# Layer 0's MLP output on the seven-product scheme, its sums added up by transfers, modulation loads moved

## The chip, the cores and the metric

The kernel runs on one core of a Trainium2 chip. The metric is the device time of one execution in microseconds (us). Three runs of the kernel before took 2149.72, 2150.34 and 2150.58 us, median 2150.34. A difference is called measurable here where it is over 0.2% of that, 4.3 us.

A core has engines that work side by side, each through its own instruction queue in order: TensorE (PE, matrix products into the banks of PSUM), VectorE (DVE, element-wise work), ScalarE (ACT, element-wise functions), GpSimd (POOL) and SyncE (SP). The last two do little here but start transfers (DMAs).

## The reference

A two-layer encoder trunk on one sequence of 256 tokens with 2048 features, all in float32. Only its shape matters:

```python
for l in range(2):
    mod = silu(c) @ w_ada[l] + b_ada[l]                 # 2048 x 12288
    sh_a, sc_a, g_a, sh_m, sc_m, g_m = split(mod, 6)
    h = rmsnorm(x) * (1 + sc_a) + sh_a
    x = x + g_a * (attention(h) @ w_o[l])               # two groups of heads
    h = rmsnorm(x) * (1 + sc_m) + sh_m
    y = square(relu(h @ w_mlp_in[l])) @ w_mlp_out[l]    # 2048 -> 8192 -> 2048
    x = x + g_m * y
return rmsnorm(x, final_norm_g)
```

## The kernel before

**Products in parts.** A float32 matrix is split into `hi` (rounded to float32r by ACT) and `lo` (the rest, subtracted by DVE), and a product is three: hi by hi, hi by lo, lo by hi. So each weight tile of 128 by 2048 numbers (1 MB) that SP loads into a `raw` buffer costs ACT two roundings and DVE two subtractions of 128 by 1024 (`weights`, `part`, L151 and L154) before PE can use it. There are five `raw` buffers and four each of `hi` and `lo`, so loads and splits run ahead of PE by about two tiles of weights.

**The MLP.** The 8192 hidden features are worked off in four blocks (`fb` 0 to 3) of 2048. A block first makes its hidden features 128 at a time (`wides`, PE tile `ps`, L217 and L220; then `relu2` or `relu` and `split`), then multiplies them with 2048 rows of the second matrix. That second product gives 2048 output columns, in four column groups `c` of 512, for two halves `t` of the tokens. `rows` and `rows_by_k` (PE tile `pr`, L311 to L314) make one column group from four weight tiles, with 96 products of 128 by 512.

Layer 0 does so for all four column groups (`mlp`). Block 0 keeps its results in `y`, block 1 adds them (`added`), and `updates` multiplies each result with the gate row (`row`, tile `bias`) into `yg` and adds it to `x` on DVE.

Layer 1 (`block_by_seven`) makes the left half (column groups 0 and 1) differently: two by two blocks (token halves by feature halves by column groups) are multiplied with seven block products in place of eight, by sums and differences of blocks. `seven` makes the combinations for each pair of feature tiles: of the hidden features (`comb`, `sh`, `sl`) and of the weights (`comb`, 128 by 2048, L1179 to L1181). It adds its products into seven PSUM banks `pp`, p1 to p7, in two steps, `five` and `two`, that are placed between the `wides` of later tiles. At the end of a block `four` combines p1 to p7 into the four results on DVE. The right half stays with `rows_by_k`. So a block of layer 1 has two stages: one that mixes `ps` and `pp`, and one of `pr` alone (8 weight tiles, 192 products).

**Modulation.** `mod` is computed on DVE: 192 tiles of `w_ada` of 1 MB each, each multiplied and summed by one instruction (`ada_sums`, L380). The loads go through the same queue (SP) and the same five `raw` buffers as the weights. How many are started is set by `rate`: each call of `weights` adds `rate` to a credit and starts that many loads; the sums stand on DVE behind the next weight tile's splits. `ada_need` makes sure that a group is there when it is used.

**The order.** Instructions of each engine stand in program order but for what a scheduler in the recording layer exchanges, so places are shown below as the built program has them.

Of the kernel before, what the change touches and what calls it, by code (L numbers as in the profile page):

```python
# [18 lines left out]
D = 2048  # L19
# [78 lines left out]
RATE_A0, RATE_V, RATE_A1, RATE_A2, RATE_K, RATE_K1, RATE_M = 1.1, 1.6, 0.5, 0.7, 0.6, 0.0, 0.7  # L98
# [3 lines left out]
class Trunk:  # L102
    def __init__(self, ctx, tc, io):
# [4 lines left out]
        self.up = pool("up", 40)  # L108
        self.tp = pool("tp", 6)
# [190 lines left out]
    def rows_by_k(self, pss, w, xs, kq, ts=(0, 1)):  # L300
# [3 lines left out]
        for h in range(2):  # L304
            for i in range(4):
                for t in ts:
                    ps = pss[t].rearrange("p a b -> p (a b)")
                    c = slice(t * P, (t + 1) * P)
                    xh, xl, _ = xs[4 * kq + i]
# [572 lines left out]
    def layer(self, l, acc=None):  # L882
# [164 lines left out]
        self.rate = RATE_M  # L1047
        if l:
            for fb in range(NFB):
                self.block_by_seven(fb, h, banks)  # L1050
                banks = []
        else:
            self.mlp(h, banks)
        self.quiet = False

    def mlp(self, h, banks):

        io = self.io
        late = []
        for fb in range(NFB):  # L1060
            hid = []
            done = 0 if fb else 12
            for m in range(done, NK, 2):
                ps = self.wides([io["w_m10"][NK * fb + m + j - 12] for j in range(2)], h)
                for b in banks:
                    hid += self.relu2(b)
                banks = []
                hid += self.relu2(self.joined(ps, self.t("sum")))
            if fb == 1:
                self.gate(0, 5)  # L1070
            for c in range(4):
                pss = self.rows(io["w_m2"][0, fb], hid, c, fb == NFB - 1 and c == 3)
                if fb == 0:
                    late += [self.copy(ps, "y") for ps in pss]
                else:
                    if late:
                        pss = [self.added(late.pop(0), ps) for ps in pss]
                    self.updates(pss, c, fb == NFB - 1)

    def block_by_seven(self, fb, h, banks):  # L1080
# [3 lines left out]
        plain = len(banks)  # L1084
        for m in range(0, plain, 2):
            hid += self.relu2(self.joined(banks[m : m + 2], self.t("sum")))
        for m in range(plain, NK, 2):
            both = self.t("sum")
            for j in range(2):
                ps = self.wides([io["w_m11"][NK * fb + m + j - 6]], h)[0]  # L1090
                self.join(ps, both[:, j])
                if m > plain + 2:
                    steps.pop(0)()
            r = self.relu(both)
            parts = self.split(r, "hid", True)
            hid += parts
            steps += self.seven(io["w_ms"][fb, m // 2], parts, r, sums, m == plain, m == NK - 2)
        for f in steps:
            f()
        if fb == 0:  # L1100
            self.gate(1, 5)
        end = fb == NFB - 1
        done = self.final if end else self.updates
        first, adds, halves = self.four(sums)
        first()
        light = adds + [lambda c=c: done(halves[c], c) for c in range(2)]
        pss = [self.bank("pr") for _ in range(2)]
        for kq in range(4):
            self.rows_by_k(pss, self.weights(io["w_m2"][1, fb, 2, kq]), hid, kq)
            if kq < 3 or not plain:  # L1110
                light.pop(0)()
        done(pss, 2)
        if plain:
            self.both_by_k([self.weights(io["w_ms"][fb, m // 2]) for m in range(0, plain, 2)], hid, halves)
            light.pop(0)()
        if end:
            light.pop(0)()
            pss = self.rows(io["w_m2"][1, fb], hid, 3, True)
        else:
            pss = [self.bank("pr") for _ in range(2)]  # L1120
            for kq in range(4):
                self.rows_by_k(pss, self.weights(io["w_m2"][1, fb, 3, kq]), hid, kq)
                if light:
                    light.pop(0)()
        done(pss, 3)

    def both_by_k(self, ws, xs, halves):
# [15 lines left out]
        for c in range(2):  # L1143
            for t in range(2):
                y = flat(halves[c][t])
# [514 lines left out]
```

## Time and profile before

| | us |
|---|---|
| Runs (three): lowest, median, highest | 2149.72, 2150.34, 2150.58 |
| Profiled execution, first to last instruction (its span) | 2147.8 |
| Layer 0, attention and first norm (to the first `tx` of the MLP's norm) | 0 to 398 |
| Layer 0, MLP: norm and block 0; block 1; block 2; block 3 | 398 to 581; to 757; to 933; to 1109 |
| Layer 1, attention | 1109 to 1445 |
| Layer 1, MLP: norm and block 0; block 1; block 2; block 3 | 1445 to 1623; to 1795; to 1967; to 2139 |

The profile tells no time of its execution other than the span; the 2.5 us by which the median of the runs is longer lie around it. The stages are read from the timeline of PE, by the names of its output tiles. Matrix products overlap in their pipeline: a product of 128 by 512 is shown with 0.39 us, but the next starts 0.23 us later; the same holds in part for DVE and ACT.

### The profile page before, as it was taken

What the parts mean: (1) busy time and instruction counts of PE and PEld (TensorE: products, weight loads), DVE (VectorE), ACT (ScalarE), POOL (GpSimd) and SP (SyncE); (2) the same over time, 40 slices, a digit from 0 to 9 for tenths busy, and PEclk for the clock granted to TensorE, in tenths of its full rate; (3) what the DMA queues carried; (4) which work ended last, traced back from release to release, by engine and by line L of the source; (5) the groups of instructions that cost most, each with busy time, mean ns of one, the idle gap of its engine ahead of it and who ended that gap; (6) DMA issues with size and microseconds to landing.
All of it is one profiled execution on the core that took longest, in us unless ns stands there. A gap on an engine that the chain in (4) does not pass through costs nothing.

```text
span 2147.8 us, 29564 instructions
## 1 busy us (share of the span) xinstructions
PE 2122.2 (99%) x11411; PEld 1841.3 (86%) x11411; DVE 1776.3 (83%) x2444; ACT 1209.9 (56%) x1829; POOL 6.2 (0%) x18
## 2 busy tenths in 40 slices
PE   7999999999999999999999999999999999999998
PEld 6899887898888888888889998888888888888886
DVE  8889888988688888888877886778977897897897
ACT  6555663565465355345455576647645765664674
POOL 0000000000000000000000000000000000000000
PEclk9999999999999999999999999999999999999999
DMA  9989899799888888988967776776665564565553
GB/s 395 423 343 334 324 353 346 285 335 344 322 318 329 347 319 323 341 311 318 344 222 275 255 254 236 274 250 210 227 237 186 184 239 153 198 233 177 191 191 128
DMA packets 87245, 594.76 MB, mean 277 GB/s; under 512 B 9856, under 2 KB 10304, under 8 KB 20288
## 3 DMA queue, kind: packets, MB, share of 16 engines
q1 hardware_dynamic: 85536, 586.41, 73.9%
q0 software_dynamic: 848, 5.28, 0.6%
q8 instruction: 89, 1.46, 0.3%
q10 hardware_dynamic: 720, 1.19, 0.2%
q14 instruction: 52, 0.43, 0.1%
HBM read 589.66 MB, written 3.18 MB: 276 GB/s over the span
## 4 chain that ended last, share of the span: by engine, by line
PE 92%; DVE 3%; DMA 2%; ACT 2%; issue 1%; ACTq 0%; DVEq 0%
PE ps L217 19%; PE pr L311 10%; PE pr L314 10%; PE pr L312 10%; PE ps L220 10%; PE pk L260 3%; PE pk L284 2%; PE pk L194 2%; PE pk L198 2%; PE pk L197 2%; PE pp L1171 2%; PE pp L1170 2%; PE pp L1172 2%; PE pv L298 2%; PE pv L296 2%; PE pv L297 2%
## 5 line engine op out<-in xcount | busy, mean ns | idle before, releaser
L151 ACT ACTIVATE hi<-raw 128x1024 fp32r<-128x1024 f32 (+2 forms) x714 | 720.1, 1019 | 617.0 <-PE pr L312 275.6
L154 DVE TENSOR_TENSOR lo<-raw,hi 128x1024 fp32r<-128x1024 f32 (+2 forms) x714 | 821.1, 1171 | 261.8 <-issue 105.5
L380 DVE SCALAR_TENSOR_TENSOR ada<-ada,cond 128x2048 f32<-128x2048 f32 x192 | 438.2, 2284 | 13.8 <-DMA ada<-in_w_ada 13.1
L217 PE MATMUL ps<-h,hi 128*128 128x512 f32 x1856 | 436.5, 390 | 0.0
L217 PEld LDWEIGHTS ps<-h,hi 128*128 128x128 f32 x1856 | 345.2, 188 | 71.1 <-DVE sum L1367 1.3
L311 PE MATMUL pr<-hi,hid 128*128 128x512 f32 x768 | 298.9, 389 | 0.0
L312 PE MATMUL pr<-hi,hid 128*128 128x512 f32 x768 | 298.8, 389 | 0.0
L220 PEld LDWEIGHTS ps<-h,lo 128*128 128x128 f32 x1856 | 234.2, 191 | 6.8
L220 PE MATMUL ps<-h,lo 128*128 128x256 f32 x1856 | 236.2, 283 | 0.0
L314 PE MATMUL pr<-lo,hid 128*128 128x512 f32 x768 | 190.3, 389 | 0.0
L312 PEld LDWEIGHTS pr<-hi,hid 128*128 128x128 f32 x768 | 144.2, 188 | 29.9
L314 PEld LDWEIGHTS pr<-lo,hid 128*128 128x128 f32 x768 | 144.1, 188 | 29.9
L311 PEld LDWEIGHTS pr<-hi,hid 128*128 128x128 f32 x768 | 144.1, 188 | 29.8
L1366 ACT ACTIVATE sum<-ps 128x256 f32<-128x256 f32 x110 | 42.0, 382 | 87.4 <-PE ps L220 86.8
L194 PE MATMUL pk<-h,hi 128*128 128x256 f32 x320 | 90.4, 285 | 0.2 <-ACT h L715 0.2
L198 PE MATMUL pk<-h,lo 128*128 128x256 f32 x320 | 90.5, 283 | 0.0
L197 PE MATMUL pk<-h,hi 128*128 128x256 f32 x320 | 90.5, 283 | 0.0
L260 PE MATMUL pk<-hf,w 128*128 128x256 f32 x384 | 83.9, 379 | 0.0
L260 PEld LDWEIGHTS pk<-hf,w 128*128 128x128 f32 x384 | 72.8, 190 | 9.9
L154 DVE TENSOR_TENSOR lo<-comb,hi 128x1024 fp32r<-128x1024 f32 x58 | 70.4, 1218 | 6.3 <-PE ps L220 6.3
L151 ACT ACTIVATE hi<-comb 128x1024 fp32r<-128x1024 f32 x58 | 60.7, 1052 | 8.5 <-PE pp L1172 5.5
L194 PEld LDWEIGHTS pk<-h,hi 128*128 128x128 f32 x320 | 61.2, 192 | 0.6 <-ACT h L715 0.5
(288 smaller groups left out, 3129.2 us busy)
## 6 DMA issues: line engine op xcount, KB each, us to landing
raw<-in_w_m SPq DMA_DIRECT2D x206, 1024.0 KB, 5.9
ada<-in_w_ada SPq DMA_DIRECT2D x192, 1024.0 KB, 6.5
raw<-in_w_o SPq DMA_DIRECT2D x32, 1024.0 KB, 5.7
raw<-in_w_ms SPq DMA_DIRECT2D x32, 1024.0 KB, 5.0
raw<-in_w_m SPq DMA_DIRECT2D x24, 768.0 KB, 5.4
raw<-in_w_dv SPq DMA_DIRECT2D x16, 1024.0 KB, 5.8
raw<-in_w_t SPq DMA_DIRECT2D x12, 1024.0 KB, 5.0
w<-in_w_a SPq DMA_DIRECT2D x24, 384.0 KB, 13.5
```

The source lines that it names most:

```text
L151: ins = self.nc.scalar.activation(hi, v, AF.Copy)
L154: ins = self.nc.vector.tensor_tensor(lo, v, hi.bitcast(F32), ALU.subtract)
L194: ins = mm(ps, hi, x[0], start=first, stop=False, skip_group_check=shared)
L197: mm(ps, hi, x[1], start=False, stop=False, skip_group_check=shared)
L198: self.last_mac = mm(ps, lo, x[0], start=False, stop=last, skip_group_check=shared)
L217: mm(ps.rearrange("p a b -> p (a b)"), part(w, k, 0), x[2], start=k == 0, stop=False)
L220: mm(ps[:, 0], part(w, k, 1), x[0], start=False, stop=k == nk - 1)
L260: self.nc.tensor.matmul(ps, v, whole[k], start=first, stop=last, skip_group_check=True)
L311: mm(ps, xh[:, c], part(i, 0), start=kq == 0 and i == 0, stop=False)
L312: mm(ps, xl[:, c], part(i, 0), start=False, stop=False)
L314: self.last_mm = mm(ps, xh[:, c], part(i, 1), start=False, stop=kq == 3 and i == 3)
L380: ins = nc.vector.scalar_tensor_tensor(w, w, 1.0, self.cond, ALU.mult, ALU.mult, accum_out=acc[:, i : i + 1])
```

## The change

- **Layer 0, blocks 1 to 3** go through `block_by_seven`: the left half of the second product by seven block products, as in layer 1. Block 0 (`first_block`) stays with `rows`.
- **The sums p1 to p7 are kept over the blocks** of a layer in seven tiles `acc` in the memory SBUF, and combined once, at the end of block 3 (`merged`, seven additions on DVE). In the blocks between, ACT copies each bank into a tile `part`, and a transfer that POOL starts adds it to `acc` (`gather`); in block 3 DVE adds the banks (`gather` with `end`). Block 0's left half goes into `acc` as p2, p3, p4, p7 (layer 0: by copies and one subtraction; layer 1: by `both_by_k`, as before for the tiles that `wide_by_k` made).
- **Gated rows of the right half** are multiplied with the gate on DVE and added to `x` by such a transfer (`add_late`), for blocks 1 and 2 and, in the next block's first stage, for block 0. Block 3 adds on DVE (`updates`, `final`), the left half of all blocks with it.
- **Modulation loads** start at other rates: none in the `ps`/`pp` stages of layer 0, 1.25 for each weight tile in the `pr` stages, 1.0 in block 0, more in layer 1's attention (0.7 and 1.2 for 0.5 and 0.7), 0.3 in the first stage of layer 1's block 0.
- Hidden features are split in one instruction of 512 columns in place of two of 256. Pools: `u` 44 for 40 tiles, `t` 8 for 6; the memory for transfers that POOL starts shrinks to 4096 bytes of each partition.

```diff
-RATE_A0, RATE_V, RATE_A1, RATE_A2, RATE_K, RATE_K1, RATE_M = 1.1, 1.6, 0.5, 0.7, 0.6, 0.0, 0.7
+RATE_A0, RATE_V, RATE_A1, RATE_A2, RATE_K, RATE_K1, RATE_M0, RATE_R = 1.1, 1.6, 0.7, 1.2, 0.6, 0.4, 1.0, 1.25
+RATE_S = 0.0, 0.3
...
-        if l:
-            for fb in range(NFB):
-                self.block_by_seven(fb, h, banks)
-                banks = []
-        else:
-            self.mlp(h, banks)
+        acc, late = ({}, []) if l else self.first_block(h, banks)
+        for fb in range(1 - l, NFB):
+            self.block_by_seven(l, fb, h, banks if l and fb == 0 else [], acc, late)
...
     def block_by_seven(self, l, fb, h, banks, acc, late):
...
+            if fb == 1 and m == 2:
+                self.gate(l, 5)
+            while m > 4 and late:
+                self.add_late(*late.pop(0))
...
+        self.rate = RATE_R
         end = fb == NFB - 1
-        done = self.final if end else self.updates
-        first, adds, halves = self.four(sums)
-        first()
-        light = adds + [lambda c=c: done(halves[c], c) for c in range(2)]
+        light = [lambda g=g: self.gather(acc, sums, g, end) for g in ((1, 2), (3, 5), (7, 6), (4,))]
+        halves = []
+        if end:
+            done = self.final if l else lambda pss, c: self.updates(pss, c, True)
+            light += [lambda: halves.extend(self.merged(acc))]
+            light += [lambda c=c: done(halves[c], c) for c in range(2)]
+        elif fb:
+            def done(pss, c):
+                for t in range(2):
+                    self.add_late(pss[t], t, c)
...
+    def gather(self, acc, sums, group, end):
+        flat = lambda v: v.rearrange("p a b -> p (a b)")
+        for i in group:
+            ps = sums[i - 1]
+            if i not in acc:
+                acc[i] = self.copy(ps, "acc")
+            elif end:
+                self.nc.vector.tensor_tensor(acc[i], ps, acc[i], ALU.add)
+            else:
+                t = self.t("part")
+                self.nc.scalar.activation(t, ps, AF.Copy)
+                self.nc.gpsimd.dma_start(flat(acc[i]), flat(t), accum_op=ALU.add)
+
+    def add_late(self, y, t, c):
+        tmp = self.t("yg").rearrange("p a b -> p (a b)")
+        self.nc.vector.tensor_tensor(
+            tmp, y.rearrange("p a b -> p (a b)"), self.row[:, 512 * c : 512 * c + 512], ALU.mult
+        )
+        self.nc.gpsimd.dma_start(self.xs_of(t, c), tmp, accum_op=ALU.add)
+
+    def merged(self, acc):
+        op = self.nc.vector.tensor_tensor
+        a1, a2, a3, a4, a5, a6, a7 = [acc[i] for i in range(1, 8)]
+        op(a6, a1, a6, ALU.add)
+        op(a2, a1, a2, ALU.add)
+        op(a7, a6, a7, ALU.add)
+        op(a4, a7, a4, ALU.subtract)
+        op(a6, a6, a5, ALU.add)
+        op(a3, a6, a3, ALU.add)
+        op(a5, a7, a5, ALU.add)
+        return [a2, a4], [a3, a5]
...
-        return self.split(self.relu(ps), "hid", True)
+        return self.split(self.relu(ps), "hid")
...
-    nc = bacc.Bacc("TRN2", target_bir_lowering=False, num_devices=1)
+    nc = bacc.Bacc("TRN2", target_bir_lowering=False, num_devices=1, dynamic_dma_scratch_size=4096)
```

**DVE, last stage of layer 0's block 3.** These rows of the kernel before stand in the middle of the stage, between two weight tiles (`lo` are the splits of weights, `ada` the sums of the modulation, `yg` and `x` the gated update):

```order
L154 TENSOR_TENSOR lo_9358<-raw_9355,hi_9357 128x1024
L154 TENSOR_TENSOR lo_9362<-raw_9355,hi_9361 128x1024
L154 TENSOR_TENSOR lo_9406<-raw_9403,hi_9405 128x1024
L154 TENSOR_TENSOR lo_9410<-raw_9403,hi_9409 128x1024
L380 SCALAR_TENSOR_TENSOR ada_9365,macc_94<-ada_9365,cond 128x2048
L394 TENSOR_TENSOR mod_93<-macc_94,vec 128x2
L154 TENSOR_TENSOR lo_9444<-raw_9441,hi_9443 128x1024
L1288 TENSOR_TENSOR yg_9391<-pr_9243,bias 128x512
```

At the same place the changed kernel has, between the last split of one weight tile and the first of the next (`acc` are the kept sums):

```order
L155 TENSOR_TENSOR lo_9782<-raw_9775,hi_9781 128x1024
L381 SCALAR_TENSOR_TENSOR ada_9748,macc_88<-ada_9748,cond 128x2048
L1160 TENSOR_TENSOR acc_6645<-acc_6553,acc_6645 128x512
L395 TENSOR_TENSOR mod_87<-macc_88,vec 128x2
L1161 TENSOR_TENSOR acc_4852<-acc_6553,acc_4852 128x512
L1162 TENSOR_TENSOR acc_5010<-acc_6645,acc_5010 128x512
L1303 TENSOR_TENSOR yg_9820<-acc_4852,bias 128x512
L1163 TENSOR_TENSOR acc_4854<-acc_5010,acc_4854 128x512
L1164 TENSOR_TENSOR acc_6645<-acc_6645,acc_6601 128x512
L1305 TENSOR_TENSOR x<-x,yg_9820 128x512
L1165 TENSOR_TENSOR acc_5008<-acc_6645,acc_5008 128x512
L1166 TENSOR_TENSOR acc_6601<-acc_5010,acc_6601 128x512
```

Ahead of the next weight tile now stand the merge, part of the update of the left half, and a modulation sum. From the stage's last `sl` split to the split `lo_9942` in its next-to-last weight tile, DVE's queue holds 15 splits of weights of 128 by 1024, 7 modulation sums, 26 additions and multiplications of 128 by 512 (7 `gather`, 7 `merged`, 12 for `yg` and `x`) and 4 small ones; between the first uses of the same two tiles PE's queue holds 173 products of 128 by 512.

**SP, last stage of a middle block in layer 0.** Loads of the kernel before, in block 2:

```order
L170 DMA raw_6242<-in_w_m 128x2048
L364 DMA ada_6253<-in_w_ada 128x2048
L170 DMA raw_6279<-in_w_m 128x2048
L170 DMA raw_6325<-in_w_m 128x2048
L364 DMA ada_6335<-in_w_ada 128x2048
```

and of the changed kernel, at the beginning of that stage in block 2:

```order
L171 DMA raw_8109<-in_w_m 128x2048
L365 DMA ada_8119<-in_w_ada 128x2048
L365 DMA ada_8121<-in_w_ada 128x2048
L171 DMA raw_8153<-in_w_m 128x2048
L365 DMA ada_8166<-in_w_ada 128x2048
L171 DMA raw_8198<-in_w_m 128x2048
L365 DMA ada_8209<-in_w_ada 128x2048
L171 DMA raw_8238<-in_w_m 128x2048
```

Overall, the queue of SP starts 88 modulation loads in layer 0's MLP before and 56 now (28 with block 0 and the norm, 10, 10 and 8 in the `pr` stages), 28 in layer 1's attention before and 47 now (17 of them with the 16 tiles of `w_o`, before 10), and 2 in layer 1's MLP before and 15 now, in its norm and block 0; layer 0's attention keeps its 74.

**POOL, same stage.** Before, POOL's queue has only the gate rows here; now, for block 2 of layer 0:

```order
L1146 DMA acc_6553<-part_8101 128x512
L1146 DMA acc_4852<-part_8104 128x512
L1146 DMA acc_5008<-part_8147 128x512
L1146 DMA acc_6601<-part_8150 128x512
L1146 DMA acc_5010<-part_8192 128x512
L1146 DMA acc_6645<-part_8195 128x512
L1146 DMA acc_4854<-part_8235 128x512
L1154 DMA x<-yg_8276 128x512
L1154 DMA x<-yg_8279 128x512
L1154 DMA x<-yg_8437 128x512
L1154 DMA x<-yg_8440 128x512
```

Eleven transfers of 256 KB that add to what lies at their target now run beside that stage's 18 loads of 1 MB; block 1 has eight.

113 lines of the change are left out of this document (47 added, 66 removed).

## The prediction

> **What bounds the kernel now.** I read the page's busy times and its chain of waits first, then the stages by windows, then the order of work in time at the places that the change touches. The page (busy time, share of the span, instructions; then the chain's shares by engine):
>
> ```profile
> PE 2122.2 (99%) x11411; PEld 1841.3 (86%) x11411; DVE 1776.3 (83%) x2444; ACT 1209.9 (56%) x1829; POOL 6.2 (0%) x18
> ...
> PE 92%; DVE 3%; DMA 2%; ACT 2%; issue 1%; ACTq 0%; DVEq 0%
> ```
>
> PE is busy in 99% of the span and carries 92% of the chain, so time is saved only where PE gets fewer or shorter products, and lost wherever something makes PE wait. DVE with 83% is the engine with the least to spare. The windows by stage (length, busy us and instructions of PE, PEld, DVE, ACT, POOL, clock, DMA share, GB/s), in layer 0 the last stage of block 0, the two stages of block 1, blocks 2 and 3, then layer 1's blocks 1 and 2:
>
> ```profile
> 494.00:581.10 87.10, 87.10 (x387) 72.11 (x386) 64.59 (x65) 39.94 (x45) 0.00 (x0) 1.00 0.93 345
> 581.10:670.00 88.90, 88.90 (x515) 78.74 (x513) 70.97 (x89) 51.30 (x77) 0.00 (x0) 1.00 0.85 311
> 670.00:757.20 87.20, 87.20 (x387) 72.21 (x386) 76.29 (x85) 35.91 (x38) 1.05 (x2) 1.00 0.88 345
> 757.20:933.10 175.90, 175.90 (x898) 150.78 (x897) 146.49 (x170) 86.55 (x112) 0.00 (x0) 1.00 0.87 324
> 933.10:1109.00 175.90, 175.90 (x897) 150.72 (x896) 140.94 (x168) 88.20 (x125) 0.00 (x0) 1.00 0.83 306
> ...
> 1623.20:1795.30 172.10, 171.69 (x874) 145.80 (x873) 145.06 (x200) 104.47 (x137) 0.00 (x0) 1.00 0.55 196
> 1795.30:1967.30 172.00, 171.59 (x874) 145.79 (x873) 145.03 (x200) 104.48 (x137) 0.00 (x0) 1.00 0.55 196
> ```
>
> PE never idles in layer 0's blocks, at the full clock. Layer 1's blocks, which do the same mathematics with seven products for eight, are 3.9 us shorter. But DVE is as busy there (145 us) with no modulation sums at all as in layer 0 with some 22 of them. That is the question of this change: it saves PE products and needs DVE time that layer 0 spends on modulation.
>
> **The saving.** Three blocks of layer 0 take the form of layer 1's. From the rows, 176.1, 175.9 and 175.9 us become 172.0 or 172.1 each: 527.9 less 516.2, **-11.7 us**. This is less than the products alone (24 fewer in each block at 0.227 us, 5.4 us), since it holds the short waits that a seven-product block has. It stands only if DVE, ACT and transfers keep up as in layer 1; the next terms are what is different.
>
> **The debt of DVE in layer 0's block 3.** Durations of DVE and PE as they follow each other, from start to next start:
>
> ```profile
> 1052.31 2.28 DVE L380 SCALAR_TENSOR_TENSOR ada<-ada,cond 128x2048 f32<-128x2048 f32 x1
> 1054.52 0.08 DVE L380 DVE_READ_ACCUMULATOR ada<-ada,cond 128x1 f32 x1
> 1054.52 2.35 DVE L154 TENSOR_TENSOR lo<-raw,hi 128x1024 fp32r<-128x1024 f32 x2
> ...
> 2097.25 0.68 DVE L1210 TENSOR_TENSOR y<-pp,y 128x512 f32<-128x512 f32 x1
> 2097.85 2.35 DVE L154 TENSOR_TENSOR lo<-raw,hi 128x1024 fp32r<-128x1024 f32 x2
> 2100.11 0.68 DVE L1213 TENSOR_TENSOR y<-pp,y 128x512 f32<-128x512 f32 x1
> ...
> 2095.76 0.39 PE L311 MATMUL pr<-hi,hid 128*128 128x512 f32 x1
> 2095.99 0.39 PE L312 MATMUL pr<-hi,hid 128*128 128x512 f32 x1
> ```
>
> A modulation sum holds DVE for 2.21 us (1052.31 to 1054.52), a split of 1024 columns 1.13 (2097.85 to 2100.11 for two), an addition of 512 columns 0.60 (2097.25 to 2097.85), a product PE for 0.2275. The order of the changed kernel gives the counts between the stage's last `sl` and `lo_9942`: DVE 15 x 1.13 + 7 x 2.21 + 26 x 0.60 + 4 x 0.1 = 17.0 + 15.5 + 15.6 + 0.4 = 48.5 us, PE 173 x 0.2275 = 39.4 us. DVE needs 9.1 us more than PE. Whether PE waits for all of it depends on the lead with which DVE begins. The same place in layer 1's block 3 shows the lead:
>
> ```profile
> 2091.20 0.50 PE L1171 MATMUL pp<-lo,hid 128*128 128x512 f32 x1 [0.17 <-DVE lo L154]
> 2092.42 0.50 PE L1170 MATMUL pp<-hi,sh 128*128 128x512 f32 x1 [0.24 <-ACT sh L1161]
> ...
> 2093.54 0.68 DVE L1162 TENSOR_TENSOR sl<-comb,sh 128x512 fp32r<-128x512 f32 x1
> ...
> 2094.37 0.40 PE L1172 MATMUL pp<-hi,sl 128*128 128x512 f32 x1
> ```
>
> PE already waits for DVE and ACT there, and the last `sl` (done at 2094.22) is used 0.15 us later: the end of the first stage uses up the lead. Bounds: 5 us, if some lead is left (4 us, a weight tile's splits ahead), to 11 us, if modulation sums also wait for their loads. I take **+9.1**. Behind the splits wait the updates of `x`, and behind these the norm of layer 1.
>
> **Middle blocks: transfers.** In the `pr` stage of blocks 1 and 2 DVE has 16 splits, 10 sums and 4 gate products, 18.1 + 22.1 + 2.4 = 42.6 us against 192 x 0.2275 = 43.7 us of PE: full, without a debt. Transfers are another matter. Two windows, of a stage at the transfers' limit and of layer 0's `w_o`, and the issues (KB each, median us to landing):
>
> ```profile
> 60.00:70.00 10.00, 10.00 (x47) 8.61 (x46) 9.97 (x17) 7.87 (x15) 0.00 (x0) 1.00 1.02 422
> 300.00:398.00 98.00, 95.97 (x428) 77.77 (x427) 87.12 (x105) 50.45 (x89) 1.18 (x2) 1.00 0.91 351
> ...
> ada<-in_w_ada SPq DMA_DIRECT2D x192, 1024.0 KB, 6.5
> ...
> bias<-gate POOLq DMA_DIRECT2D x4, 1024.0 KB, 8.1
> ...
> out_y<-x SPq DMA_DIRECT2D x6, 256.0 KB, 2.1
> ```
>
> At 422 GB/s the engines are full. The stage's 18 loads of 1.05 MB alone take 44.7 us, over its 43.7. The adding transfers (eight in block 1, eleven in block 2) are not in the trace; the nearest rows are stores of the same 256 KB. If each costs one pass of 0.26 MB, 0.62 us, the sum is 49.7 and 51.5 us, if two, 54.6 and 58.3; so transfers fall 6 to 15 us behind. What covers it: three of the five `raw` buffers are loaded when the stage begins (7.5 us), and loading goes on in the last 5 us of the stage before, so that at the last weight tile some 0 to 6 us are late; the five `ps` tiles that follow need only 1.05 MB in 5.6 us, and catch up. A gain is excluded: PE had no idle time there. I take 1 us for block 1 and 2 for block 2, **+3** (bounds 0 and 9), near the low end, because layer 0's `w_o` stage, with nearly one modulation load for each weight tile, lost 2.0 us (98.00 less 95.97). The Trainium skill, "DMA: Bandwidth & Descriptors", section "Rules for kernel authors", says that spreading DMAs over SP, ACT and GpSimd brings no bandwidth, since all run on the same 16 engines. By that rule the additions moved off DVE are paid again here; were they apart from the loads, this term would be 0 to 1 and the sum 2 us lower.
>
> **Layer 1's attention.** It gets 19 sums more, 42 us of DVE, 7 of them beside `w_o` (the two windows of before, and PE's waits in layer 0's `w_o` stage):
>
> ```profile
> 1203.80:1352.00 148.20, 148.20 (x962) 136.17 (x961) 115.61 (x214) 98.45 (x190) 0.00 (x0) 1.00 0.69 242
> 1352.00:1444.70 92.70, 92.70 (x420) 76.96 (x419) 68.17 (x83) 46.26 (x79) 1.05 (x2) 1.00 0.76 272
> ...
> PE pr L311 <- ACT hi L151: 2.0, 3, 1.0
> ```
>
> Its `w_o` stage goes from 68.2 to 68.2 + 7 x 2.21 = 83.7 of 92.7 us of DVE, 90%, as in layer 0 (87.1 of 98.0, 89%), where PE waited 2.0 us. So 2 there and 1 ahead of it, **+3** (0 to 6).
>
> **Layer 1's norm and block 0** get 13 sums more, 28.7 us, and lose the combination, the left half's updates and the right half's additions to `x`, (7 + 8 + 4) x 0.60 = 11.4 us. The last row is layer 1's last stage:
>
> ```profile
> 1449.00:1623.20 174.20, 173.94 (x883) 148.14 (x884) 147.49 (x212) 107.58 (x154) 1.05 (x2) 1.00 0.64 231
> ...
> 2095.80:2147.80 52.00, 43.65 (x193) 35.81 (x191) 38.03 (x53) 23.23 (x37) 0.00 (x0) 0.94 0.32 119
> ```
>
> 147.5 + 28.7 - 11.4 = 165 of 174.2 us, 95%: **+1.5** (0 to 4). **Layer 1's blocks 1 and 2** lose the same 11.4 us of DVE each, but PE idles there only 0.4 us in a block (172.10 less 171.69), so this brings **-0.5** in all (0 to -0.8). Block 3 has seven additions more, 4.2 us, in a stage in which DVE is busy 38.0 of 52.0: nothing; without that cover it would be the 4.2. Block 0 of layer 0 has some six sums more, 13 us, which the idle 22.5 of 87.1 us hide, and the wider splits save a little on DVE and ACT, hidden behind PE.
>
> **Sum.** -11.7 + 9.1 + 3 + 3 + 1.5 - 0.5 = +4.4 us. The profiled execution has a span of 2147.8, which becomes 2152.2; the 2.5 us around it that the median of the runs (2150.34) has on top stay: **2155 us**, rounded up. All lower ends together give 2143, all upper ends 2169. Changes under 0.2%, 4.3 us, can't be told from none.
>
> **The rivals.**
>
> *DVE's lead covers the debt: faster.* There are four `hi` and four `lo` buffers, two weight tiles or 10.9 us of PE. If DVE comes to the last stage that far ahead, the 9.1 us vanish; the first stage of layer 0's blocks has no modulation sums now, and the wider splits help. Then -11.7 with 0 to 9 us of the rest: 2139 to 2148, likeliest 2143. Against it stand the rows at 2091 to 2094, where the lead was gone without any sum. It decides at a lead of 5 us at the last `sl`. Chance 0.33.
>
> *Transfers set the pace: slower.* If the adding transfers cost two passes and lengthen every landing, blocks 1 and 2 wait the upper 9 us, and the late sums lengthen the debt to 11: 2162 to 2170. The 6.5 us to landing of the loads speak for it, the free stretch behind each stage against it. The Trainium skill, "Collectives: The Full Stack", section "The bandwidth ceiling: the fold count and why AG ≠ RS ≠ AR", says that an adding transfer is slow by its two source reads, not by the addition. No trace here shows one yet; by this rule the upper price holds. Chance 0.16.
>
> *The tiles `part` and `yg` come free late: slower.* They lie in the eight `t` tiles until an adding transfer has landed, and ACT and DVE need the same tiles. With 8 us to landing, as `bias<-gate` has, four are held at most; from about 20 us on, ACT would wait for one in each stage, some 3 us in each of three to five stages: 2165. On POOL itself only more such transfers and the gate rows, needed later, stand behind one that waits. Chance 0.05.
>
> *The change doesn't save what it says.* PE's queue is 72 products shorter in the built program, so this could only be by the clock or a second wait: no difference, 0.04.
>
> **Numbers.** The forecast has 0.42, its own range 2149 to 2161 (0.15 of it within 0.2%, 0.27 slower). Faster: 0.28 (the first rival, whose other 0.05 is within 0.2%); same: 0.15 + 0.05 + 0.04 = 0.24; slower: 0.27 + 0.16 + 0.05 = 0.48. Range 2140 to 2166: it leaves out the lowest part of the first rival and the upper parts of the second and third.
>
> **What would show it.** The PE chain should have layer 0's blocks 1 and 2 at 172 to 175 us and block 3 at about 181, with PE waiting in its last stage for `lo`, and DVE without a gap there. If block 3 takes 172 to 175 us, the lead was misjudged. In blocks 1 and 2 waits for `hi` whose own wait ended with a load speak for the transfers. Layer 1's `w_o` stage should lose 2 us. The prediction is wrong if DVE idles in block 3's last stage, or if an adding transfer takes far longer than 3 us of the engines' time.

## The result and the profile after

| | before | after |
|---|---|---|
| median of the runs, us | 2150.22 (4 runs, 2149.72 to 2150.58) | 2184.07 (4 runs, 2182.99 to 2185.57) |
| span of the profiled execution, us | 2147.8 | 2182.5 |

The changed kernel is slower: ratio 1.0159, 95% interval 1.0145 to 1.0173, some 34 us. The page of the changed kernel (busy time, share of the span, instructions; the queue that GpSimd's transfers use, with packets, MB and share of 16 engines' span; the chain's shares by engine):

```profile
PE 2125.5 (97%) x11339; PEld 1828.8 (84%) x11339; DVE 1868.8 (86%) x2558; ACT 1268.2 (58%) x1872; POOL 49.7 (2%) x67
...
q0 software_dynamic: 7904, 18.12, 3.9%
...
PE 81%; DVE 9%; DMA 6%; ACT 2%; issue 1%; ACTq 0%; DVEq 0%
```

PE has 72 instructions fewer, and its share of the chain falls from 92% to 81%: DVE and DMA have come onto it. The windows of layer 0's blocks 1, 2 and 3, each split into the hidden part (`ps` and `pp`) and the last stage (`pr`):

```profile
584.20:711.40 127.20, 127.12 (x679) 109.22 (x678) 115.59 (x160) 88.79 (x118) 5.51 (x7) 1.00 0.64 225
711.40:763.40 52.00, 45.54 (x198) 36.46 (x197) 40.36 (x41) 18.32 (x22) 4.37 (x5) 1.00 1.02 374
763.40:891.80 128.40, 128.30 (x682) 109.75 (x681) 116.45 (x159) 88.27 (x117) 3.56 (x4) 1.00 0.60 214
891.80:948.00 56.20, 48.20 (x194) 37.85 (x193) 39.08 (x40) 19.12 (x22) 6.22 (x7) 0.94 1.03 357
948.00:1077.40 129.40, 128.81 (x682) 109.65 (x681) 116.37 (x160) 84.83 (x111) 1.77 (x2) 1.00 0.59 208
1077.40:1131.70 54.30, 48.12 (x194) 37.70 (x193) 51.50 (x64) 20.73 (x31) 0.00 (x0) 0.94 0.83 294
```

The reader is to see three things. The hidden parts run at PE's pace. The last stages, which have 43.7 us of products (192 x 0.2275), take 52, 56 and 54. And the last columns part them: in blocks 1 and 2 the DMA engines are busy all the time while DVE is busy 39 or 40 us; in block 3 the DMA engines have room and DVE is busy 51.5 of 54.3. The column before the DMA share is the clock that TensorE was granted: 0.94 in the last stages of blocks 2 and 3, full elsewhere; what that is worth is shown with the reasons below.

By the stretches between PE's `pr` products, the 34.8 us come from here:

| stretch | before | after | difference |
|---|---|---|---|
| up to the end of layer 0's block 0 | 581.2 | 584.3 | +3.1 |
| layer 0's block 1 | 176.1 | 179.2 | +3.1 |
| block 2 | 175.9 | 184.6 | +8.7 |
| block 3 | 176.0 | 183.7 | +7.7 |
| layer 1's norm and attention, up to `w_o` | 243.0 | 245.5 | +2.5 |
| its `w_o` stage | 92.6 | 97.5 | +4.9 |
| norm and block 0 of its MLP | 178.5 | 184.4 | +5.9 |
| the rest | 516.1 | 515.0 | -1.1 |

What PE waits for in two of these stretches (engine, line, waited for: us in total, times, longest). Block 2's last stage, then block 3's:

```profile
ACT hi L152 <- DMA raw<-in_w_m: 31.4, 7, 7.9
...
PEld pr L312 <- ACT hi L152: 10.1, 5, 3.0
PE pr L312 <- ACT hi L152: 8.0, 5, 2.5
```

```profile
PEld pr L315 <- DVE lo L155: 7.1, 4, 3.1
PE pr L315 <- DVE lo L155: 5.4, 4, 2.6
```

In block 2 PE waits for `hi`, whose own wait ends with a load; in block 3 for `lo`. The chain of waits inside block 2's last stage (start, us, what) shows the same as time:

```profile
892.79 10.54 DMA raw<-in_w_m
906.98 11.64 DMA raw<-in_w_m
...
925.60 8.52 DMA raw<-in_w_m
```

A load of 1 MB takes 2.49 us of all the engines' time (1.05 MB at the 422 GB/s of the prediction's row) and lands after 6.3 us at the median in this kernel; here it is 8.5 to 11.6 us on its way. Its competitors are modulation loads and adding transfers. Their price can be read from the queue: 3.9% less the 0.6% of before, of 2182.5 us, over 49 adding transfers, is 72 / 49 = **1.47 us of all 16 engines** for 256 KB.

### The profile page after: what moved, and what is told of

It is laid out like the page before. It is cut to its first block, busy times and chain, and to the rows that moved or that the text cites. A ratio compares the mean times of both kernels' runs of the same rounds, so it can differ in the third digit from the quotient of the medians.

```text
span 2182.5 us, 29752 instructions
## 1 busy us (share of the span) xinstructions
PE 2125.5 (97%) x11339; PEld 1828.8 (84%) x11339; DVE 1868.8 (86%) x2558; ACT 1268.2 (58%) x1872; POOL 49.7 (2%) x67
## 3 DMA queue, kind: packets, MB, share of 16 engines
q0 software_dynamic: 7904, 18.12, 3.9%
q8 instruction: 89, 1.46, 0.2%
## 4 chain that ended last, share of the span: by engine, by line
PE 81%; DVE 9%; DMA 6%; ACT 2%; issue 1%; ACTq 0%; DVEq 0%
PE ps L218 18%; PE ps L221 10%; PE pr L312 6%; PE pr L313 6%; PE pr L315 6%; DVE lo L155 4%; DMA raw<-in_w_m 3%; PE pk L261 3%; PE pp L1216 3%; PE pp L1215 3%; PE pp L1214 3%; DVE ada L381 2%; PE pk L195 2%; PE pk L199 2%; PE pk L198 2%; PE pk L285 2%
## 5 line engine op out<-in xcount | busy, mean ns | idle before, releaser
L312 PE MATMUL pr<-hi,hidh 128*128 128x512 f32 x576 | 229.4, 398 | 17.5 <-ACT hi L152 17.3
L313 PE MATMUL pr<-hi,hidl 128*128 128x512 f32 x576 | 227.2, 395 | 0.0
L312 PEld LDWEIGHTS pr<-hi,hidh 128*128 128x128 f32 x576 | 110.0, 191 | 47.8 <-ACT hi L152 25.0
L315 PE MATMUL pr<-lo,hidh 128*128 128x512 f32 x576 | 144.7, 392 | 5.4 <-DVE lo L155 5.4
L155 DVE TENSOR_TENSOR lo<-comb,hi 128x1024 fp32r<-128x1024 f32 x106 | 128.9, 1218 | 7.7 <-PE ps L221 7.2
L315 PEld LDWEIGHTS pr<-lo,hidh 128*128 128x128 f32 x576 | 108.4, 189 | 29.5 <-DVE lo L155 7.1
L313 PEld LDWEIGHTS pr<-hi,hidl 128*128 128x128 f32 x576 | 110.1, 191 | 22.8
L152 ACT ACTIVATE hi<-comb 128x1024 fp32r<-128x1024 f32 x106 | 111.4, 1054 | 24.5 <-PE pp L1216 14.7
L1215 PE MATMUL pp<-lo,sh 128*128 128x512 f32 x212 | 83.4, 393 | 0.2 <-DVE lo L155 0.2
L1214 PE MATMUL pp<-hi,sh 128*128 128x512 f32 x212 | 81.9, 394 | 1.0 <-ACT sh L1205 1.0
```

What stands on the lines that cost most here:

```text
L152: ins = self.nc.scalar.activation(hi, v, AF.Copy)
L155: ins = self.nc.vector.tensor_tensor(lo, v, hi.bitcast(F32), ALU.subtract)
L312: mm(ps, xh[:, c], part(i, 0), start=kq == 0 and i == 0, stop=False)
L313: mm(ps, xl[:, c], part(i, 0), start=False, stop=False)
L315: self.last_mm = mm(ps, xh[:, c], part(i, 1), start=False, stop=kq == 3 and i == 3)
L1214: nc.tensor.matmul(ps, x[0], wh, start=first, stop=False)
```

## The experiments

In each comparison the kernel before, run beside, took 2150.1 to 2150.8 us. Each kernel here ran once, k_two2 apart, which was timed again. One thing limits single comparisons: the stretch up to the last stage of layer 0's block 0, which the edits hardly touch, ends anywhere from 492.6 to 497.9. So totals are read to 2 or 3 us, single stages more closely.

Theory T: in blocks 1 and 2 the DMA engines set the pace, with modulation loads and adding transfers together. Theory S: layer 1's loss is the price of the modulation that the change moved there. The rivals stand with the runs. The stages of all runs, in us (last stages of layer 0's blocks 1, 2, 3; then layer 1's `w_o` stage, and norm with block 0 of its MLP; then the time):

| kernel | 1 | 2 | 3 | `w_o` | block 0 | time |
|---|---|---|---|---|---|---|
| the changed kernel | 52.2 | 56.4 | 54.4 | 97.5 | 184.4 | 2184.1 |
| a_plain | 49.7 | 50.7 | 54.4 | 97.6 | 184.5 | 2175.6 |
| b_noada | 44.6 | 43.7 | 43.7 | 96.9 | 191.9 | 2206.2 |
| c_gdve | 48.3 | 48.6 | 52.8 | 97.5 | 185.7 | 2173.0 |
| d_alldve | 46.9 | 47.8 | 54.4 | 97.7 | 185.7 | 2182.3 |
| h_l1less | 51.7 | 56.4 | 52.8 | 92.6 | 178.8 | 2170.2 |
| f_even | 45.5 | 45.5 | 46.6 | 93.9 | 197.8 | 2174.5 |
| k_two | 45.5 | 51.3 | old form | 92.6 | 181.8 | 2157.3 |
| k_one | 47.8 | old form | old form | 92.6 | 181.6 | 2156.1 |
| p_pool | 50.4 | 50.9 | 52.8 | 99.1 | 187.0 | 2192.8 |
| k_two2 | 45.5 | 45.6 | old form | 92.6 | 181.1 | 2146.9 |
| k_two3 | 45.5 | 50.7 | old form | 92.6 | 181.0 | 2165.0 |

**a_plain: transfers that don't add.** Both helpers' transfers lose the addition:

```diff
-                self.nc.gpsimd.dma_start(flat(acc[i]), flat(t), accum_op=ALU.add)
+                self.nc.gpsimd.dma_start(flat(acc[i]), flat(t))
...
-        self.nc.gpsimd.dma_start(self.xs_of(t, c), tmp, accum_op=ALU.add)
+        self.nc.gpsimd.dma_start(self.xs_of(t, c), tmp)
```

> Both adding transfers lose their addition and become plain copies of the same 256 KB between the same places, so the sums of blocks 1 and 2 and the rows added late are left out of the result; every load, sum, gate and product stays where it is. Theory T (the 16 DMA engines set the pace of the last stage of layer 0's blocks 1 and 2, and an adding transfer of 1.47 us of their time weighs 2.4 plain ones): block 2's last stage has about 9 of them inside, each 0.85 us shorter, so 56.2 us becomes about 48.5 (46 to 51) and block 1's 52.0 about 48; block 3 stays at 54 because its debt is VectorE's; in all 2184 becomes 2168 to 2175. Rival M (1.25 modulation loads per weight tile, with 44.8 us of loads against 43.7 us of products and a VectorE sum behind each load, fill the stage without the adding transfers): the two stages stay within 1.5 us of 52.0 and 56.2, time 2180 to 2186.

Block 2 lost 5.7 us, block 1 2.5, block 3 nothing. Rival M falls in its pure form, and T's numbers were a little too good (50.7 against 48.5, 2175.6 against 2168 to 2175). The same queue's row in this kernel:

```profile
q0 software_dynamic: 4768, 18.12, 2.1%
```

2.1% less 0.6%, of 2173.8 us, over 49 is 0.67 us. So the addition makes a transfer of the same bytes 2.2 times as costly for the engines. The Trainium skill, "Collectives: The Full Stack", section "The bandwidth ceiling: the fold count and why AG ≠ RS ≠ AR", puts the slowness of a reduce-scatter, whose steps add, down to the two source reads of the addition; the factor here agrees with that in size, and no run shows the reads themselves.

**b_noada: no modulation in the last stages of layer 0.**

```diff
-        self.rate = RATE_R
+        self.rate = RATE_R if l else 0.0
```

> No modulation loads or sums in the last stage of layer 0's blocks 1 to 3 (rate 0 there); some 30 of them are forced later, ahead of layer 1's norm, which gets longer by some 30 x 2.49 = 75 us, so the total is no comparison and only the three stages count. T: with adding transfers and no modulation loads the DMA engines have 8 x 2.49 + 11 x 1.47 = 36 us of work in 43.7 us, so blocks 1 and 2 fall to 44 to 46 us; block 3 too, because 10 sums of 2.21 us leave VectorE (51.5 us becomes 29). M: the same 44 to 46. A third theory, B (the burst of seven adding transfers at the stage's head blocks the weight loads behind it by itself): 3 to 6 us stay, 48 to 52 us.

All three stages run at PE's pace: 44.6 (with four products of the left half among them), 43.7 and 43.7 us. The adding transfers are all still there, in the same burst at the stage's head, so theory B falls: by themselves they cost nothing. Layer 1's blocks 1 and 2 of the changed kernel, with the same transfers and no modulation, had said so (last stages of 44.6 and 43.7). This run also confirms the saving: a seven-product block without modulation takes 171.5 to 172 us. And it shows what block 3's debt was, in the window of that block's last stage:

```profile
1055.50:1099.20 43.70, 43.70 (x195) 36.16 (x194) 42.98 (x56) 20.74 (x31) 0.00 (x0) 1.00 0.74 255
```

DVE is busy in 42.98 of 43.70 us, not in the 29 that were expected, and yet PE waits for nothing. Four modulation sums are still in the stage, loaded for layer 1; but the first starts at 1085.61, in the stage's last 14 us, behind most of the splits. In the changed kernel seven sums stand in the stage, the first two at 1083.03 and 1085.24, 6 and 8 us after its beginning, between the splits that PE needs next. So the debt comes of the sums that stand ahead of splits, and not of DVE being full by itself.

**c_gdve and d_alldve: VectorE adds.** In the first the seven sums of every block are added by DVE, in the second also the late rows:

```diff
-            elif end:
+            elif True:
                 self.nc.vector.tensor_tensor(acc[i], ps, acc[i], ALU.add)
```

> The seven sums of a block are added by VectorE from their banks (7 x 0.60 us) in every block, as the change does in the last block only; the late rows still go by adding transfer. T: 7 x 1.47 = 10.3 us of DMA time leave block 2's stage and 5.9 us (4 sums) block 1's, but 4.2 us come to VectorE, which was busy 39.1 of 56.2 us there: 46 to 50 us in both. M: VectorE's part of the pace grows, so 56 stays or gets longer, 54 to 60. B: 46 to 50, as T. Total by T 2165 to 2178.

> No adding transfer is left: sums and late rows are both added by VectorE. T: 18 x 2.49 = 44.8 us of loads in block 2's last stage and VectorE at about 39 + 7 = 46 us: 46 to 49 us; what is gained over the one with VectorE's sums alone is small (0 to 2 us), since most late rows are added outside of the stage. M: 52 to 58. Total by T 2163 to 2178; layer 1's blocks 1 and 2, which have adding transfers but no modulation loads, stay at 171 to 173 us by every theory unless VectorE falls behind there.

Blocks 1 and 2 fell as T said, to 48.3 and 48.6, then 46.9 and 47.8. The second kernel's total was a miss: 2182, not 2163 to 2178. Its late rows fall on DVE in the hidden parts, whose lengths went from 126.9 to 130.5 us in block 1 of layer 0 and from 126.7 to 130.1 in block 1 of layer 1; the stretch up to block 1 of layer 0 was also 3 us longer, within what unaltered code shows. So DVE has no room for these additions there, and moving them to transfers was worth something.

The five variants can be put beside one sum. Block 2 has 18 loads at 2.49 us, 44.8 us, and about nine transfers inside its last stage:

| kernel | transfers' sum, us | measured, us |
|---|---|---|
| changed | 44.8 + 9 x 1.47 = 58.0 | 56.4 |
| a_plain | 44.8 + 9 x 0.67 = 50.8 | 50.7 |
| c_gdve | 44.8 + 2 x 1.47 = 47.7 | 48.6 |
| d_alldve | 44.8 | 47.8 |
| b_noada | 19.9 + 9 x 1.47 = 33.1 | 43.7, PE's pace |

The stage takes about the transfers' sum or PE's time, whichever is longer. d_alldve, with no adding transfer left, lies 3 us above its sum; DVE is busy there 44.3 of 47.8 us, which may be why, but it was not isolated. p_pool, below, has the same sum of 44.8 and took 50.9, beside additions that slow DVE.

**h_l1less: layer 1 without the moved modulation.** The rates of before, and the constants that stand for the scale and gate of layer 1's MLP:

```diff
-RATE_A0, RATE_V, RATE_A1, RATE_A2, RATE_K, RATE_K1, RATE_M0, RATE_R = 1.1, 1.6, 0.7, 1.2, 0.6, 0.4, 1.0, 1.25
+RATE_A0, RATE_V, RATE_A1, RATE_A2, RATE_K, RATE_K1, RATE_M0, RATE_R = 1.1, 1.6, 0.5, 0.7, 0.6, 0.0, 1.0, 1.25
...
+        self.ada_todo = [x for x in self.ada_todo if x[:2] not in ((1, 4), (1, 5))]
+        self.nc.gpsimd.memset(self.mod[1, 4], 1.0)
+        self.nc.gpsimd.memset(self.mod[1, 5], 1.0)
```

> Layer 0 stays as changed. In layer 1 the rates of before stand (0.5, 0.7 and 0 ahead of the MLP), and the 32 modulation tiles of the scale and the gate of its MLP, as many as the change moved into layer 1, are left out (constants stand for them), so that nothing is forced later. Theory S (layer 1's 13 us are the price of 32 moved loads and sums, about 0.4 us each): norm and attention 245.6 becomes 243.0, the last products of the attention 97.5 becomes 92.6, norm and block 0 of the MLP 184.3 becomes 178.5; in all 2184 becomes 2169 to 2172. Rival U (layer 1's loss comes of its MLP's sums being gathered in tiles that hold buffers of the common pool, or of the new order, not of the modulation): norm and attention as S says, but the MLP's block 0 stays at 182 to 184, in all 2174 to 2177.

S as stated: 243.7, 92.6 and 178.8 us, 2170.2 in all; U falls. The `w_o` stage of layer 1 in the changed kernel, and in this one:

```profile
1382.00:1474.70 92.70, 89.72 (x398) 73.99 (x397) 81.04 (x96) 40.86 (x68) 0.55 (x1) 0.98 0.90 336
```

```profile
1373.50:1466.10 92.60, 92.60 (x420) 77.02 (x419) 67.58 (x83) 46.01 (x79) 1.06 (x2) 1.00 0.75 269
```

With 9 sums (counted by `ada` in DVE's records) PE is never idle. The other runs point to room that is used up, rather than to a price for each sum: 92.6 us with up to 13 sums in this stage, 97.5 with 16. With 15 it was 93.9 in f_even and 96.9 in b_noada, so the count alone doesn't settle it. What PE waited for in the changed kernel, near the end of this stage:

```profile
ACT hi L152 <- DMA raw<-in_w_o: 10.7, 3, 7.2
...
PE pr L312 <- ACT hi L152: 3.0, 1, 3.0
```

It waits for `hi`, and `hi` for a load of `w_o`: the loads are late here too, as in the middle blocks.

**f_even: the loads spread, the transfers kept.**

```diff
-RATE_S = 0.0, 0.3
+RATE_S = 0.3, 0.6
...
-        self.rate = RATE_R
+        self.rate = RATE_R if l else (0.0, 0.5, 0.5, 0.25)[fb]
```

> The adding transfers stay; layer 0's modulation loads are spread: in blocks 1 to 3 0.3 per weight tile in the hidden part (0 before) and 0.5, 0.5 and 0.25 in the last stage (1.25 before). Theory T (the loads and adding transfers of the last stage add up to more than its 43.7 us of products): 13 loads x 2.49 + 9 x 1.47 = 46 us in block 2's last stage, most of it hidden since the loads may run ahead into the hidden part, so blocks 1 and 2 fall to 44 to 47 us; block 3 with 1 to 2 sums to 45 to 48; the hidden part, where VectorE was busy 116 of 128 us, takes 3 to 5 sums of 2.2 us and stays within 2 us. Layer 0's three blocks 547.5 becomes 520 to 530, the whole 2160 to 2169. If the burst of adding transfers at the stage's head is what stalls the products (theory B), 49 to 53 us stay in blocks 1 and 2, the whole 2170 to 2178.

The last stages of the three blocks, with adding transfers in the first two:

```profile
715.40:760.90 45.50, 45.50 (x202) 37.67 (x201) 33.06 (x33) 22.10 (x25) 5.22 (x6) 1.00 1.02 366
891.20:936.80 45.60, 45.60 (x202) 37.73 (x202) 33.29 (x33) 21.65 (x25) 7.13 (x8) 1.00 1.04 349
1066.00:1112.50 46.50, 46.50 (x206) 38.47 (x207) 41.86 (x55) 22.33 (x32) 0.00 (x0) 1.00 0.66 228
```

PE has no idle time left in any (45.5 us are 200 products: eight of the left half, `pp`, lie among the stage's 192). T holds: four modulation sums in each of the first two stages in place of nine, one in place of seven in the third, with all adding transfers, and 52 and 56 us are gone. The hidden part of block 1, with six sums, grew by 3.0 us, 1 more than expected. Note the DMA share of 1.02 to 1.04: a full share does not by itself mean that anyone waits. The total was a miss, 2174.5 in place of 2160 to 2169. The three blocks took 527.0 us, as expected, but layer 1's MLP block 0, into which this run's rates put 20 sums, took 197.8.

These 527.0 us are the whole story of the change in one number: the kernel before took 528.0 for the same blocks, and carried 65 modulation sums there, where this one carries 25 (both counted in DVE's records between the `pr` products). The products saved are paid for with room for some 40 sums, which then have to find a place elsewhere.

**k_two and k_one: seven products in fewer blocks.** The remaining blocks of layer 0 go by the plain products of before at 0.7 modulation loads per weight tile, and add the merged sums to their first two column blocks:

```diff
...
-            self.block_by_seven(l, fb, h, banks if l and fb == 0 else [], acc, late)
+            if l == 0 and fb >= 3:
+                self.block_old(fb, h, acc)
+            else:
+                self.block_by_seven(l, fb, h, banks if l and fb == 0 else [], acc, late)
...
```

This is k_two; k_one has `fb >= 2`. `block_old` and the rates are left out here.

> Seven products only in layer 0's blocks 1 and 2; block 3 goes by the plain products of before, takes the sums of the others into its first two column blocks, and carries 0.7 modulation loads per weight tile again; blocks 1 and 2 carry 0.15 and 0.55, and layer 1 somewhat fewer than with the change. Theory S with T (a block on the seven products saves 4.4 us, and what it cannot carry of the modulation costs about 0.4 us per sum elsewhere): blocks 1 and 2 at 172 to 174 us each, block 3 at 176 to 178, layer 1 loses about 8 us in place of 13: 2150 to 2158, within a few us of the kernel before. Rival: the adding transfers keep a price of their own, blocks 1 and 2 at 177 or more: 2160 to 2168.

> Seven products only in layer 0's block 1, blocks 2 and 3 by the plain products with 0.7 modulation loads per weight tile; layer 1's rates near those of before (0.6, 0.9 and 0.25). S with T: block 1 at 172 to 173, blocks 2 and 3 at 176 to 177 each, block 0 within 1 us, layer 1 loses 3 to 5 us: 2146 to 2153. If the price of moved sums is not what makes layer 1 slow, it loses the 13 us again, and the whole is 2156 to 2163.

2157.3 and 2156.1: most of the 34 us are gone. k_two came out at the upper end of what S with T said, k_one 3 us above it, at the edge of its rival. The rival's reason is not the one: layer 1 lost 1.5 us ahead of `w_o`, nothing in it and 3.1 in block 0, the 3 to 5 us of S. But the last seven-product block lost time, 51.3 and 47.8 us with only five and four sums. The waits in k_two's block 2, and in k_one's block 1:

```profile
DVE acc L1183 <- DMA acc<-part: 6.7, 1, 6.7
...
PE pr L316 <- DVE lo L156: 3.5, 1, 3.5
```

```profile
DVE acc L1185 <- DMA acc<-part: 8.3, 1, 8.3
```

That is a new wait, of my making: the merge of the seven sums follows in DVE's queue and stands there until the last adding transfer has landed, with the `lo` splits queued behind it.

**p_pool: GpSimd adds by itself.**

```diff
-                self.nc.gpsimd.dma_start(flat(acc[i]), flat(t), accum_op=ALU.add)
+                self.nc.gpsimd.tensor_tensor(acc[i], acc[i], t, ALU.add)
```

> GpSimd adds the same operands itself, in place of giving the addition to an adding transfer: no transfer is left in either helper, ScalarE's copies, VectorE's gating and every load stay. Theory T (the room that adding transfers take on the DMA engines): blocks 1 and 2's last stages fall to what the kernel without any adding transfer showed, 46 to 48 us, and with less VectorE work than that one; block 3 stays at 53 to 54; in all 2184 becomes 2168 to 2174. Rival V (GpSimd's additions take turns with VectorE's at the buffers): the mean of VectorE's lo subtraction goes above 1.25 us in these stages, they stay at 49 to 56 us, and layer 1's blocks 1 to 3 get longer than 172 us; in all 2178 to 2195.

V: 2192.8 us, within its 2178 to 2195, and slower than with adding transfers or with DVE's own additions. The group of these additions (line, operation, count, busy us and mean ns of one), and DVE beside four of them at 642.33 to 652.90, in the hidden part of block 1:

```profile
L1146 POOL TENSOR_TENSOR acc<-acc,part 128x512 f32<-128x512 f32 x25 | 67.2, 2720 | 370.8 <-ACT part L1145 370.8
```

```profile
642.33 10.57 POOL L1154 TENSOR_TENSOR x<-x,yg 128x512 f32<-128x512 f32 x4 [32.52 <-DVE yg L1151]
```

```profile
645.25 2.00 DVE L155 TENSOR_TENSOR lo<-comb,hi 128x1024 fp32r<-128x1024 f32 x1
647.17 4.56 DVE L155 TENSOR_TENSOR lo<-raw,hi 128x1024 fp32r<-128x1024 f32 x2
651.65 2.33 DVE L155 TENSOR_TENSOR lo<-comb,hi 128x1024 fp32r<-128x1024 f32 x1
653.91 1.21 DVE L155 TENSOR_TENSOR lo<-raw,hi 128x1024 fp32r<-128x1024 f32 x1
```

A split that takes 1.21 us alone takes 2.0 to 2.3 while GpSimd adds. The hidden part grew from 126.9 to 133.6 us. In the last stages of blocks 1 and 2 the mean of the split rose from 1.22 to 1.41 and 1.46 us, as V said, and in block 2's DVE was busy 47.2 of 50.9 us; still they were shorter than with adding transfers (50.4 and 50.9 for 52.2 and 56.4). The loss was mostly in the hidden parts of block 1 in both layers, in layer 1 132.3 us for 126.7. Of layer 1's blocks, which V had above 172 us, only block 1 was, with 176.9.

**k_two2 and k_two3.** Both have seven products in blocks 1 and 2 alone, with 0.75 modulation loads per weight tile in their last stages and lower rates in layer 1; in k_two2 DVE adds the sums of block 2, so that the merge needs no landing; in k_two3 GpSimd adds all. The line that k_two2 has beyond k_two, other than rates:

```diff
-        light = [lambda g=g: self.gather(acc, sums, g, end) for g in ((1, 2), (3, 5), (7, 6), (4,))]
+        light = [lambda g=g: self.gather(acc, sums, g, end or (l == 0 and fb == 2)) for g in ((1, 2), (3, 5), (7, 6), (4,))]
```

> As with seven products in blocks 1 and 2 alone, but block 2's seven sums are added by VectorE, so that the merging of the sums in the following block finds them there and does not hold VectorE for an adding transfer's landing (6.7 us in that kernel), and blocks 1 and 2 carry 0.75 modulation loads per weight tile in the last stage in place of 0.55, layer 1 some 4 less. S with T: block 2's last stage 51.3 becomes 44 to 46, block 1's 45 to 47, layer 1 1 to 2 us less: 2148 to 2153. If the wait for the landing was not what held the stage, 51 stays and the whole is 2155 to 2158.

> The same with all sums and late rows added by GpSimd. T: no adding transfer and no VectorE work for the sums, block 1 and 2's last stages at 44 to 45: 2146 to 2151. V: VectorE's operations get longer beside GpSimd's, 2152 to 2162.

k_two2 came out at 2146.9, block 2's stage at 45.6: the wait for the landing had been what held it. The edit also took seven adding transfers out of that stage; but f_even had all of them there, with four sums and no merge behind them, and took 45.5, so their time on the engines was not what held it. k_two3, at 2165, is p_pool's loss again (block 1's hidden part 133.1 us, block 2's last stage 50.7). The same kernel as k_two2 was then timed:

> The kernel with seven products in layer 0's blocks 1 and 2 alone, VectorE's sums in block 2 and spread modulation loads, timed against the kernel before. If S with T holds, the 3.8 us of the single run stand: 2146 to 2149 against 2150.2, a ratio of 0.998 to 0.9995. If the single run was a fortunate one: 2149 to 2153, no difference.

2148.6 us against 2150.78, ratio 0.9992, interval 0.9983 to 1.0001. So it is 35 us faster than the change, and not told apart from the kernel before; the 3.8 us of the single run don't stand.

## Why the prediction was wrong

It said slower, by 4.4 us in span, and it was 34.7. Its steps:

- **The saving, -11.7: right.** Without modulation the blocks take 171.5 to 172 us, 4 us less than before (b_noada).
- **DVE's debt in block 3, +9.1: right in mechanism and nearly in size.** 54.4 less 43.7 is 10.7 us, with PE waiting for `lo` and DVE without a gap (busy in all of the 52.34 us from the last `sl`, at 1074.36), and it goes when the sums ahead of the splits go. The first rival, a lead of DVE that covers it, did not show. But the size came out partly by luck, since the sum left out the clock. Here is the same stage, first in c_gdve and then in d_alldve, with the same DVE work:

```profile
1066.00:1118.90 52.90, 47.02 (x195) 36.83 (x195) 51.61 (x65) 20.83 (x31) 0.00 (x0) 0.97 0.84 301
```

```profile
1070.30:1124.80 54.50, 48.59 (x195) 37.92 (x195) 51.58 (x65) 20.81 (x31) 0.00 (x0) 0.94 0.83 295
```

  In the traces the clock is halved for one stretch of 3.41 us in c_gdve, h_l1less and p_pool, which took 52.8 us, and for two in the changed kernel, a_plain and d_alldve, which took 54.4. By that difference, 1.6 us for a stretch, an estimate is that some 3 of the 10.7 us go with the clock and 7 to 8 are the waits; no run sets the clock by itself. In block 2's last stage it is worth nothing: 56.4 us with two such stretches (the changed kernel) and with three (h_l1less).
- **Transfers in the middle blocks, +3: this is the step that failed.** It measured 8.5 + 12.7 = 21.2 us against the products' time, and against the 172 us that the prediction set for each block, 7.1 + 12.6 = 19.7. The price was bounded rightly: at two passes the prediction had 54.6 and 58.3 us of transfers, and the stages took 52.2 and 56.4. What failed was the cover that was set against it (three `raw` buffers loaded ahead, loading in the last 5 us of the stage before, the five tiles behind) and with it the choice of 1 and 2 us, near the low end. Here is the queue that issues the loads, at the head of block 2's last stage, which begins at 891.8:

```profile
876.44 0.33 SPq L171 DMA_DIRECT2D raw<-in_w_m  x1
880.52 3.70 SPq L365 DMA_DIRECT2D ada<-in_w_ada  x2
886.84 0.33 SPq L171 DMA_DIRECT2D raw<-in_w_m  x1
890.55 0.33 SPq L365 DMA_DIRECT2D ada<-in_w_ada  x1
892.79 0.33 SPq L171 DMA_DIRECT2D raw<-in_w_m  x1
```

  Of what was ahead, more than half were modulation tiles, which PE doesn't read; of the stage's eight weight tiles two had been issued. A buffer full of the competitor's load is no lead. The comparison that led to the low end, layer 0's `w_o` stage with its 2.0 us, has no adding transfers and about one modulation load for each weight tile, where block 2's stage has ten for eight. It was also read too low: 2.0 is PE's idle time alone, but with the same 420 products the stage took 96.2 us in layer 0 (16 sums) and 92.6 in layer 1 (9 sums), so it lost 3.6.
- **The rival "transfers set the pace", 2162 to 2170: the right mechanism, still too small.** It let the loss end at the upper bound of 9 us, which rested on the same cover.
- **Layer 1's attention, +3 (0 to 6): +7.4.** The `w_o` stage lost 4.9 where 2 was taken, from that same reading; h_l1less shows it to be the moved modulation, and the waits show late loads, not the share of DVE by which the prediction judged. **Its norm and block 0, +1.5: +5.9**, of the same cause. DVE's share, 95% by the prediction's sum, was read as nearly enough room; 20 sums in f_even cost 19 us there, 21 in b_noada 13.
- **Layer 1's blocks, -0.5: -1.1**, right in sign. **Layer 0's block 0, nothing: about +3** up to its end, of which 2.6 in its last stage, with a DMA share of 0.98 where it was 0.93. a_plain, equal up to there, shows 0.3 at that point. But in all kernels with this code that stage took 88.4 to 91.0 us, where it was 87.2. It was not isolated; the five sums more, with their loads, are the likely cause, and part of the 3 us is variation between executions.
- **The tiles `part` and `yg`: no part.** The transfers of `part` took 12.9 us at the median to land, where 8 were reckoned with. But no wait for a free `t` tile stands in the quoted waits, and f_even, with the same tiles and transfers, has no idle PE in these stages.

What stays open: how the 21 us split between loads and adding transfers can't be given as two numbers, since either alone fits in (b_noada without the loads, d_alldve without the transfers but for 3 to 4 us). It is their sum that passes the limit.

## What to carry to other kernels

Price work moved to transfers in the time of all DMA engines and add it to the loads of that very stage; where the sum is above the products' time, take the difference as the loss, and don't count on buffers ahead unless the trace shows that they hold the critical tile. When a change removes work from the bottleneck engine, ask what other work was being carried in the time removed: here 12 us of products also held the room for some 40 sums. Moving an addition to another engine pays only after looking at what it slows beside it, and who stands behind its landing.

## What the runs showed of the hardware

An adding transfer of 256 KB between on-chip tiles takes 1.47 us of all 16 DMA engines, the same copy without the addition 0.67; it goes as 144 packets in place of 80 (7904 and 4768, each less 848, over 49), and the median time to landing falls from 12.9 to 8.2 us for `acc<-part` without the addition. The issues (KB each, median us to landing) of the changed kernel and of a_plain:

```profile
acc<-part POOLq DMA_DIRECT2D x25, 256.0 KB, 12.9
```

```profile
acc<-part POOLq DMA_DIRECT2D x25, 256.0 KB, 8.2
```

After waits of PE in these stages the granted clock was halved for stretches of 3.41 us; in block 3's last stage a second stretch came with 1.6 us more, in block 2's, where transfers set the pace, a third with none. GpSimd's own addition of 128x512 takes 1.9 to 2.7 us on the mean where DVE's took 0.60, and DVE's splits beside it nearly double, from 1.21 to 2.0 or 2.3 us.
